# Two pairs of output-projection tiles by seven quarter products, in a hand-set order

## The chip, the cores and the metric

The kernel runs on one core of a Trainium2 chip. A core has five engines that work beside each other: TensorE (PE; its weight loads are listed apart as PEld), VectorE (DVE), ScalarE (ACT), GpSimd (POOL) and SyncE (SP), which here only issues DMA transfers. Each engine takes its own instructions in order and waits at semaphores for the others. The metric is device time in microseconds (us) of one execution; lower is better.

## The reference

One trunk layer of a decoder, on 512 prompt tokens and 8 x 8 sample tokens, 576 tokens in all, with a model width of 1024. What matters here is the middle of the layer:

```python
yb = o @ w_attn_out                                      # attention projection
mixed = jax.nn.sigmoid(ga) * ya + jax.nn.sigmoid(gb) * yb
x = x + g1 * (mixed @ w_mix_out)                         # output projection
h2 = _rmsnorm(x, norm2_g) * (1.0 + sc2) + sh2
a, val = jnp.split(h2 @ w_up, 2, axis=-1)                # first FFN product
```

`o` (the attention's output), `ya` (the other branch) and the gates `ga`, `gb` are there by then. The last parts of the adaLN modulation, `silu(c) @ w_ada`, from which `g1`, `sc2`, `sh2` and `g2` come, are still worked out beside the attention projection. All data are float32.

## The kernel before

Activations lie with the model width on the partitions, as 8 tiles of 128 x 576 tokens. Every float32 operand is split into a high and a low part (ACT copies the high part, rounded; DVE subtracts it for the low part), and a product takes three passes a k-step: high x high, high weights x low tokens, low weights x high tokens. Weight tiles are 128 output columns by the whole depth of 1024 (512 KB), loaded by SP into `raw` and split into `whi` and `wlo`. `W_BUFS` raw tiles and `S_BUFS` split ones are there at a time, and 57 general slots of 128 x 576 (`A_BUFS`) hold everything else.

A product of one tile comes in three forms:

- `product(w, xs)`: 8 k-steps of three passes, each in two matmuls of 256 and 320 columns (the token groups `GRP`), into one of the two `mm` PSUM tiles.
- `product_g(w, xs, g)`: the same for one token group, into one of the four `aux` PSUM tiles; it can call something between two k-steps.
- `pair_product`: two tiles at once. Weights and tokens are cut in halves (depth 512, 288 tokens), and seven products of a quarter take the place of eight, in the manner of Strassen and Winograd; each is a part of 4 k-steps x 3 passes of 288 columns. It needs sums of the weight halves (`pair_weights`, whose steps `sums1`, `ah`, `al` and so on make them one by one) and of the token halves (`PairOperands`: `sums`, `high`, `low`, `n3`), and further additions on the results. The gate projections before this stage and the FFN's up tiles from 4 on already run so; the output projection doesn't.

The order of the work is set in two ways. Where an engine's wrapper (`pe`, `act`, `dve`, `pool`) is in the list `pinned`, its instructions stay in program order. Elsewhere a scheduler orders them, by its own model of times. In the attention projection `pinned.clear()` frees everything after tile 3; `pinned.append(pe)` and, later, that of DVE and ACT at `NORM2[4]` bring the fixed order back. SP, the `load` helper aside, is never pinned here, and POOL's queue carries the two loads of x1.

The stages around the change, in order:

1. Attention projection: `product` of tiles 0 to 7 with the operands `o`. After each, DVE multiplies the result with the gate (`sg<-mm,sg`), adds `ya` (`sg<-sg,ya`), and the sum is split into `mxh` and `mxl`. In between, a filler (`fill`, `tick`) puts in the adaLN work: sides of 16 matmuls over 64 weight tiles `ada` of 256 KB, and at the end the transposes that bring the modulation to columns (`modT`).
2. Output projection, tiles 0 to 4: `product` with the operands `mixed`, each followed by `residual` (scaled by `g1`, added to `x1`) and `squares` (their sums over tiles go to `acc`, for the second norm). Among them are 22 small transposes of the FFN's convolution state.
3. Output projection, tiles 5 to 7, by groups (`mix_late`): group 0 of 5, 6, 7, then group 1 of 5, 6, 7, whose weights were split into general slots ahead (`late`). In group 1 of tile 5, behind k-step `NORM2[0]`, the row sums for the norm of group 0 are taken (`norm2_rows(0)`: DVE scales, POOL takes the root), and at k-step `NORM2[1]` of the next product their result is spread over the partitions (`spread_group`).
4. The FFN's start: the first up products, with the norm of group 1 put in.

Of the kernel before, what the change touches and what calls it, by code (L numbers as in the profile page):

```python
# [10 lines left out]
F32 = mybir.dt.float32  # L11
F32R = mybir.dt.float32r
# [4 lines left out]
P = 128  # L17
# [52 lines left out]
def step_kernel(ctx: ExitStack, tc: tile.TileContext, ins: dict, outs: list):  # L70
# [40 lines left out]

            return call

    pe, act, dve, pool = (InOrder(e) for e in (nc.tensor, nc.scalar, nc.vector, nc.gpsimd))
    pinned += [pe, act, dve, pool]
    matmul, transpose = pe.matmul, pe.transpose

# [27 lines left out]
    def load_w(src, nk):  # L145

        raw = wp.tile([P, nk, P], F32, tag="raw", name=nm("raw"), bufs=W_BUFS)
        nc.sync.dma_start(raw, src)
        return raw

    def split_w(raw):
        nk = raw.shape[1]
        hi = wp.tile([P, nk, P], F32R, tag="whi", name=nm("whi"), bufs=S_BUFS)
        lo = wp.tile([P, nk, P], F32R, tag="wlo", name=nm("wlo"), bufs=S_BUFS)
        split(hi, lo, raw)
        return (lambda k: hi[:, k, :]), (lambda k: lo[:, k, :])

    def split_w_slots(raw):

# [43 lines left out]
    def halves(ps):  # L203
        return ps[:, 256:512], ps[:, 512:832]

    def product(w, xs):
        ps = mmps()
        for k in range(len(xs)):
            kstep(halves(ps), w, xs, k)
            tick()  # L210
        return pf(ps)
# [17 lines left out]
    class PairOperands:  # L229

        def __init__(self, x, kp, made, values=None):
            self.x, self.kp = (x[kp], x[kp + 4]), kp
            self.r = values and (values[kp], values[kp + 4])
            self.made = made

        def sums(self):
            if not self.r:
# [11 lines left out]
        def high(self):  # L251
            made, (h0, l0), (h1, l1) = self.made, *self.x
            self.th, self.tl = slot("th", F32R), slot("tl", F32R)
            act.activation(self.th, self.t, AF.Copy)
            if self.kp % 2 == 0:
                made["n4"] = slot("nh", F32R), slot("nl", F32R)
            a, b = slice(0, HT), slice(HT, NT)
            at = (a, b)[self.kp % 2]
            nh, nl = made["n4"]
            self.nh, self.nl = nh[:, at], nl[:, at]  # L260
            act.activation(self.nh, self.r[0][:, a], AF.Copy)
            for name, hi, lo, c in (
                ("x00", h0, l0, a), ("n3", h0, l0, b), ("x10", h1, l1, a), ("x11", h1, l1, b),
                ("n1", self.th, self.tl, a), ("t2", self.th, self.tl, b), ("n4", nh, nl, at),
            ):
                made.setdefault("op", {}).setdefault(name, []).append((hi[:, c], lo[:, c]))

        def low(self):
            for lo, src, hi in ((self.tl, self.t, self.th), (self.nl, self.r[0][:, :HT], self.nh)):
                dve.tensor_tensor(out=lo, in0=src, in1=hi.bitcast(F32), op=ALU.subtract)  # L270

        def n3(self):

            (hi, lo), b = self.x[0], slice(HT, NT)
            split(hi[:, b], lo[:, b], self.r[0][:, b])

        def all(self):
            self.sums()
# [422 lines left out]
    def state_load(src, n):  # L701
        parts = []
        for m0 in range(0, n, 4):
            c = min(4, n - m0)
            s = slot("st", shape=[P, 512])
            load(s[:16, : c * P], src.rearrange("o b r c -> (o b r) c")[:, m0 * P : (m0 + c) * P])
            parts.append(s)
        return parts

# [413 lines left out]
    def modulation(c0):  # L1123

        ps = aux()
        cols = {}

        def rows(k):
            cols[k] = [slot("ada", shape=[P, 512]) for _ in range(4)]
            for j, t in enumerate(cols[k]):  # L1130
                c = c0 + 512 * j
                nc.sync.dma_start(t, ins["w_ada"][0, k * P : k * P + P, c : c + 512])
# [28 lines left out]
        yield False  # L1161
# [165 lines left out]

    def squares(xt, m, c0=0, c1=NT):
        if m == 0:
            nc.scalar.activation(acc[:, c0:c1], xt[:, c0:c1], AF.Square)  # L1330
        else:
            sq = slot("sq")
            nc.scalar.activation(sq[:, c0:c1], xt[:, c0:c1], AF.Square)
            nc.vector.tensor_tensor(
                out=acc[:, c0:c1], in0=acc[:, c0:c1], in1=sq[:, c0:c1], op=ALU.add
            )
# [4 lines left out]
    x1t = [wp.tile([P, 4, NT], F32, tag="oh", name=nm("x1"), bufs=2) for _ in range(2)]  # L1341
    for x in range(2):
        nc.gpsimd.dma_start(x1t[x], xT_dram[x])
    x1 = [x1t[k // 4][:, k % 4, :] for k in range(NK)]
    late = []
# [78 lines left out]
    mix_late(NK - 2, 1, (NORM2[1], first_parts))  # L1424
    mix_late(NK - 1, 1)


    w_up, w_dn = ins["w_up"][0], ins["w_down"][0]

    def ffn_conv(ps, m):  # L1430
        u = padded()
# [190 lines left out]
    def w_split(raw):  # L1622
        hi, lo = (wp.tile([P, NK, P], F32R, tag=t, name=nm(t), bufs=S_BUFS) for t in ("whi", "wlo"))
        act.activation(hi, raw, AF.Copy)
        low = lambda: dve.tensor_tensor(out=lo, in0=raw, in1=hi.bitcast(F32), op=ALU.subtract)
        return ((lambda k: hi[:, k, :]), (lambda k: lo[:, k, :])), low

    def start(t, ps):
        t.copies(ps)
# [225 lines left out]
```

## Time and profile before

| | |
|---|---|
| Median of 3 runs | 1000.4 us (1000.04 to 1001.07) |
| Profiled execution | 1001.41 us, span 999.6 us |
| Mean granted TensorE clock | 0.997 |
| PE busy | 983.2 us (98%) |
| DVE, ACT, POOL busy | 67%, 45%, 10% |
| HBM read, written | 109.17 MB, 7.35 MB |

The span runs from the first to the last recorded instruction; the device time is a little more. An engine's busy share over the whole span is an average over stages with different limits, so the stages are read one by one: the windows view gives each engine's busy time in a stretch, the timeline its instructions in order of time, the waits view who waited for whom. The columns of a timeline line are start, duration (of all that are merged), engine, line, operation, output<-inputs, count, and in brackets the idle time ahead and what ended it. Most operations go through a helper, so they carry its line, L109; they are told apart by the names of their tiles.

### The profile page before, as it was taken

The page shows a single profiled execution, that of the slowest core. Times are in us where ns is not written, and L with a number is a line of the kernel's source. Part 1 is how long each engine was busy: PE and PEld are TensorE (multiplying, and loading weights), DVE is VectorE, ACT ScalarE, POOL GpSimd, SP SyncE. Part 2 cuts the span into 40 slices and gives each one's busy share as a digit, 9 for nine tenths or more (in the row PEclk, how much of TensorE's full clock was granted, in tenths as well). Part 3 has the DMA queues.
Part 4 walks back from the last instruction along what each step waited for, and adds up shares of the span by engine and source line. Part 5 has one row for each costly group of instructions (what it writes and reads, how often), then busy time and mean ns, then how long its engine had stood idle before and what let it go on. Part 6 is the DMA issues. An engine that isn't in the chain of part 4 may idle for free.

```text
span 999.6 us, 18691 instructions
## 1 busy us (share of the span) xinstructions
PE 983.2 (98%) x7516; PEld 941.8 (94%) x7516; DVE 670.7 (67%) x1241; ACT 450.8 (45%) x835; POOL 100.3 (10%) x271
## 2 busy tenths in 40 slices
PE   7999999999999999999999999999999999999997
PEld 5899999999999989999889999999999999999997
DVE  5736676676463348788454568896569995579953
ACT  5454555545334225545232347554225552235453
POOL 2221101020000000000000021011001110001120
PEclk9999999999999999999999999999999999999999
DMA  9984332233421752235972302223233222323302
GB/s 290 319 253 109 86 90 70 86 116 115 141 76 53 246 180 85 86 106 157 338 231 72 106 11 75 65 85 106 85 101 90 85 85 86 106 65 101 110 10 95
DMA packets 173481, 119.18 MB, mean 119 GB/s; under 512 B 6887, under 2 KB 160846, under 8 KB 173106
## 3 DMA queue, kind: packets, MB, share of 16 engines
q1 hardware_dynamic: 169954, 107.00, 35.3%
q0 software_dynamic: 3296, 10.73, 3.5%
q8 instruction: 59, 0.97, 0.4%
q14 instruction: 28, 0.23, 0.1%
q10 hardware_dynamic: 144, 0.26, 0.1%
HBM read 109.17 MB, written 7.35 MB: 117 GB/s over the span
## 4 chain that ended last, share of the span: by engine, by line
PE 82%; DVE 10%; issue 2%; DMA 2%; ACT 2%; SPq 0%; POOL 0%; POOLq 0%; DVEq 0%; ACTq 0%
PE mm L109 60%; PE aux L109 19%; DVE wlo L109 3%; PE aux L1116 2%; DMA ad<-in_w_ada 2%; PE aux L1016 2%; DVE raw L109 1%; DVE uv L109 1%; DVE y L109 1%; DVE cy L109 1%; DMA raw<-in_w_in 1%; DVE fl L109 1%; SPq L385 0%; DVE wl L109 0%; ACT whi L109 0%
## 5 line engine op out<-in xcount | busy, mean ns | idle before, releaser
L109 ACT ACTIVATE whi<-raw 128x1024 fp32r<-128x1024 f32 (+2 forms) x164 | 168.1, 1034 | 178.6 <-PE mm L109 95.5
L109 DVE TENSOR_TENSOR wlo<-raw,whi 128x1024 fp32r<-128x1024 f32 (+2 forms) x164 | 195.1, 1194 | 48.6 <-ACT whi L109 47.9
L109 PE MATMUL mm<-hh,whi 128*128 128x256 f32 (+2 forms) x560 | 124.6, 299 | 0.6 <-ACT hh L109 0.6
L109 PE MATMUL mm<-hh,wlo 128*128 128x256 f32 (+2 forms) x560 | 121.8, 294 | 0.0
L109 PE MATMUL mm<-hl,whi 128*128 128x256 f32 (+2 forms) x560 | 121.0, 295 | 0.1
L109 PEld LDWEIGHTS mm<-hh,whi 128*128 128x128 f32 x560 | 93.0, 188 | 2.9 <-ACT hh L109 1.2
L109 PEld LDWEIGHTS mm<-hh,wlo 128*128 128x128 f32 x560 | 94.2, 188 | 0.0
L109 PEld LDWEIGHTS mm<-hl,whi 128*128 128x128 f32 x560 | 93.6, 188 | 0.5 <-DVE hl L109 0.5
L109 DVE SCALAR_TENSOR_TENSOR x<-mm,modT,x 128x512 f32<-128x512 f32 (+1 forms) x33 | 22.6, 686 | 71.1 <-PE mm L109 71.0
L109 PE MATMUL mm<-fh,whi 128*128 128x256 f32 (+1 forms) x304 | 65.0, 296 | 0.3 <-DVE rt L109 0.3
L109 PE MATMUL mm<-fl,whi 128*128 128x256 f32 (+1 forms) x304 | 65.1, 295 | 0.0
L109 PE MATMUL mm<-fh,wlo 128*128 128x256 f32 (+1 forms) x304 | 64.9, 295 | 0.0
L109 PE MATMUL mm<-th,whi 128*128 128x288 f32 x208 | 61.7, 297 | 0.7 <-DVE uv L109 0.7
L109 PE MATMUL mm<-th,wlo 128*128 128x288 f32 x208 | 61.6, 296 | 0.6 <-DVE wlo L109 0.6
L109 PE MATMUL mm<-tl,whi 128*128 128x288 f32 x208 | 61.4, 295 | 0.0
L109 PEld LDWEIGHTS mm<-fh,whi 128*128 128x128 f32 x304 | 50.7, 188 | 0.5 <-PE mm L109 0.5
L109 PEld LDWEIGHTS mm<-fl,whi 128*128 128x128 f32 x304 | 51.0, 188 | 0.0
L109 PEld LDWEIGHTS mm<-fh,wlo 128*128 128x128 f32 x304 | 50.8, 188 | 0.0
L867 ACT ACTIVATE s<-s,nmx 128x256 f32<-128x256 f32 (+1 forms) x72 | 34.0, 474 | 32.0 <-DVE nmx L864 31.2
L109 PE MATMUL aux<-2h,whi 128*128 128x288 f32 (+2 forms) x160 | 47.2, 295 | 0.8 <-ACT p L109 0.8
L109 PE MATMUL aux<-2h,wlo 128*128 128x288 f32 (+2 forms) x160 | 47.3, 296 | 0.0
L109 PE MATMUL aux<-2l,whi 128*128 128x288 f32 (+2 forms) x160 | 47.0, 294 | 0.0
(310 smaller groups left out, 2568.8 us busy)
## 6 DMA issues: line engine op xcount, KB each, us to landing
raw<-in_w_in SPq DMA_DIRECT2D x52, 512.0 KB, 4.2
raw<-in_w_up SPq DMA_DIRECT2D x44, 512.0 KB, 3.9
ada<-in_w_ada SPq DMA_DIRECT2D x64, 256.0 KB, 6.0
ad<-in_w_ada SPq DMA_DIRECT2D x32, 256.0 KB, 6.3
raw<-in_w_down SPq DMA_DIRECT2D x16, 512.0 KB, 3.5
raw<-in_w_conv_out SPq DMA_DIRECT2D x8, 512.0 KB, 3.5
raw<-in_w_attn_out SPq DMA_DIRECT2D x8, 512.0 KB, 4.2
raw<-in_w_mix_out SPq DMA_DIRECT2D x8, 512.0 KB, 6.1
```

Of the source, the lines that this page charges most:

```text
L109: done = getattr(self.engine, name)(*args, **kwargs)
L867: nc.scalar.activation(s[x // 2][:, x % 2, :w], s[x // 2][:, x % 2, :w], AF.Exp, bias=nmx[:, x : x + 1], accum_out=den[:, x : x + 1],)
L1016: done = nc.tensor.matmul(O[HALF[par], :256], vt(i - nkt + 1 + kt)[:, hd * 64 : hd * 64 + 64], pts[kt][:, par * 256 : par * 256 + 256], st ...
L1116: done = nc.tensor.matmul(ps[32 * j : 32 * j + 32, :], cT[:, k, :], cols[k][j], start=(k == 1), stop=(k == NK - 2),)
```

## The change

- The output projection's tile 0 stays a `product`, with its k-steps in the order 0, 4, 1, 5, 2, 6, 3, 7; the state's transposes come after it. Tiles 1, 2 and tiles 3, 4 become two calls of `pair_product` (`mix_pair`). Tiles 5 to 7 stay as they are.
- The attention projection takes its tiles in the order 0, 4, 1, 5, 2, 6, 3, 7, so that after every second one a pair (kp, kp + 4) of mixed tiles is there, whose sums, high and low parts are made at once, beside the next products. With `beside=True` the operand `n3` gets slots of its own, since the plain operands are still needed. The weights of pair (1, 2) are made there too, by the steps named in `PAIR_LOW` and `PAIR_HIGH`.
- The low half of each weight split is no longer made with its high half, but one or two products ahead of its use, ahead of the multiply that follows a product.
- PE, ACT, DVE and now SP stay pinned from there on; the scheduler orders nothing of this stretch any more. The filler's rate goes from 11/60 to 11/44.
- Squares, late weights and the first three FFN weights (`ws`) are put at set places: in the pairs' steps, in `mix_late`, and ahead of the group products.
- The loads of x1 move from POOL's queue to SP's, behind the state's loads and after the fifth attention product.
- `NORM2[0]` goes from 4 to 5.

TensorE issues 24 matmuls fewer (7066 to 7042 rows of its program), DVE 54 instructions more (1225 to 1279) and ACT 20 more (740 to 760). Up to the second attention product TensorE's order is the same; from the FFN's start on the order on every engine is the same too.

The core of the diff:

```diff
-NORM2 = 4, 0, 3, 1, 3
+NORM2 = 5, 0, 3, 1, 3
+PAIR_LOW = {2: "sums1", 3: "al", 4: "dl", 5: "sums2", 6: "bl"}
+PAIR_HIGH = {2: "ah", 3: "dh", 5: "bh", 6: "ch"}
...
+    def w_split(raw):
+        hi, lo = (wp.tile([P, NK, P], F32R, tag=t, name=nm(t), bufs=S_BUFS) for t in ("whi", "wlo"))
+        act.activation(hi, raw, AF.Copy)
+        low = lambda: dve.tensor_tensor(out=lo, in0=raw, in1=hi.bitcast(F32), op=ALU.subtract)
+        return ((lambda k: hi[:, k, :]), (lambda k: lo[:, k, :])), low
...
+            if self.beside:
+                if self.kp % 2 == 0:
+                    made["n3"] = slot("nh", F32R), slot("nl", F32R)
+                self.n3_parts = [y[:, at] for y in made["n3"]]
+                act.activation(self.n3_parts[0], self.r[0][:, b], AF.Copy)
...
         else:
             w_next[0] = weights(kpm(wao, 0), NK)
-            raw = load_w(kpm(wao, P), NK)
+            raw = load_w(kpm(wao, 4 * P), NK)
...
-    filler[1] = 11 / 60
-    mixed = []
-    for m in range(NK):
-        if m + 1 < NK and m + 1 not in w_next:
-            w_next[m + 1] = weights(kpm(wao, (m + 1) * P), NK)
-        ps = product(w_next.pop(m), o)
-        if m == 3:
-            pinned.clear()
-        t = gb[m]
+    pinned.append(sync)
+    filler[1] = 11 / 44
...
+    order = [m for kp in range(4) for m in (kp, kp + 4)]
+
+    def mixed_in(m, ps, between):
+        values[m] = t = gb[m]
         dve.tensor_tensor(out=t, in0=ps, in1=t, op=ALU.mult)
         dve.tensor_tensor(out=t, in0=t, in1=ya[m], op=ALU.add)
-        mixed.append(split_slot(t, "mx"))
+        mixed[m] = hi, lo = slot("mxh", F32R), slot("mxl", F32R)
+        act.activation(hi, t, AF.Copy)
+        for step in between:
+            step()
+        dve.tensor_tensor(out=lo, in0=t, in1=hi.bitcast(F32), op=ALU.subtract)
...
+    w_high(2)
+    for i, m in enumerate(order):
+        ps = product(w_next.pop(i), o)
+        if i + 2 in lows:
+            lows.pop(i + 2)()
+        if i == 1:
+            raws = [load_w(kpm(w_mix, c * P), NK) for c in (1, 2)]
+            w_pair, steps = pair_weights(*raws)
+            del raws
+        between = [steps[n] for n in PAIR_LOW.get(i, "").split()]
+        if i and i % 2 == 0:
+            between.append(op.low)
+        mixed_in(m, ps, between)
+        if i + 3 <= NK:
+            w_high(i + 3)
+        for n in PAIR_HIGH.get(i, "").split():
+            steps[n]()
+        if i % 2:
+            op = PairOperands(mixed, i // 2, made_mix, values, beside=True)
+            op.sums()
+            op.high()
+        if i == 4:
+            ffn_state = state_load(ins["state_ffn_conv"], NF)
+            x1t = [wp.tile([P, 4, NT], F32, tag="oh", name=nm("x1"), bufs=2) for _ in range(2)]
+            for x in range(2):
+                sync.dma_start(x1t[x], xT_dram[x])
+    op.low()
+    steps["cl"]()
     drain()
...
-    stF = state_in(state_load(ins["state_ffn_conv"], NF), "stF", NF)
...
-    for x in range(2):
-        nc.gpsimd.dma_start(x1t[x], xT_dram[x])
...
-    for m in range(NK - 3):
-        w = weights(kpm(ins["w_mix_out"][0], m * P), NK)
-        if m >= NK - 6:
-            late.append(split_w_slots(load_w(kpm(ins["w_mix_out"][0], (m + 3) * P), NK)))
-        residual(product(w, mixed), x1[m], 16 + m)
-        squares(x1[m], m)
+    ps = product(w_next.pop(NK), mixed, order)
+    stF = state_in(ffn_state, "stF", NF)
+    affine(A2, 32, 56, NK)
+    residual(ps, x1[0], 16)
+    w_pair2, steps = pair_weights(*raws)
+    steps = in_turn(steps)
+    steps[5] = lambda: squares(x1[0], 0)
+    steps[6] = lambda: late_weights(5)
+    mix_pair(w_pair, 1, 2, steps)
+    steps = {
+        1: lambda: squares(x1[1], 1), 2: lambda: late_weights(6), 3: lambda: squares(x1[2], 2),
+        4: lambda: late_weights(7), 5: lambda: ws.append(first_w()),
+    }
+    mix_pair(w_pair2, 3, 4, steps)
 
     def mix_late(m, g, between=None):
         ps = product_g(late[m - NK + 3], mixed, g, between=between)
+        if (m, g) == (NK - 3, 0):
+            squares(x1[3], 3)
+            squares(x1[4], 4)
+        if (m, g) == (NK - 3, 1):
+            ws.append(first_w())
...
     for m in range(NK - 3, NK):
         mix_late(m, 0)
-    pinned.append(pe)
+    ws.append(first_w())
     mix_late(NK - 3, 1, (NORM2[0], lambda: norm2_rows(0)))
...
-    ws = [weights(kpm(w_up, c * P), NK) for c in (0, NF, 1)]
...
-            pinned.extend([dve, act])
```

More of the change, by code (lines that the diff above doesn't have):

```diff
@@ L112, in __getattr__ @@
             return call
-    pe, act, dve, pool = (InOrder(e) for e in (nc.tensor, nc.scalar, nc.vector, nc.gpsimd))
+    pe, act, dve, pool, sync = (
+        InOrder(e) for e in (nc.tensor, nc.scalar, nc.vector, nc.gpsimd, nc.sync)
+    )
     pinned += [pe, act, dve, pool]
@@ L147, in load_w @@
         raw = wp.tile([P, nk, P], F32, tag="raw", name=nm("raw"), bufs=W_BUFS)
-        nc.sync.dma_start(raw, src)
+        sync.dma_start(raw, src)
         return raw
@@ L204, in halves, with product @@
         return ps[:, 256:512], ps[:, 512:832]
-    def product(w, xs):
+    def product(w, xs, order=None):
         ps = mmps()
-        for k in range(len(xs)):
+        for k in order or range(len(xs)):
             kstep(halves(ps), w, xs, k)
@@ L229, in step_kernel, with __init__ @@
     class PairOperands:
-        def __init__(self, x, kp, made, values=None):
+        def __init__(self, x, kp, made, values=None, beside=False):
             self.x, self.kp = (x[kp], x[kp + 4]), kp
             self.r = values and (values[kp], values[kp + 4])
-            self.made = made
+            self.made, self.beside = made, beside
         def sums(self):
@@ L260, in high @@
             self.nh, self.nl = nh[:, at], nl[:, at]
+            self.n3_parts = [y[:, b] for y in (h0, l0)]
+            if self.beside:
[3 more added lines that the diff above has]
+                act.activation(self.n3_parts[0], self.r[0][:, b], AF.Copy)
+            made.setdefault("op", {}).setdefault("n3", []).append(tuple(self.n3_parts))
             act.activation(self.nh, self.r[0][:, a], AF.Copy)
             for name, hi, lo, c in (
-                ("x00", h0, l0, a), ("n3", h0, l0, b), ("x10", h1, l1, a), ("x11", h1, l1, b),
+                ("x00", h0, l0, a), ("x10", h1, l1, a), ("x11", h1, l1, b),
                 ("n1", self.th, self.tl, a), ("t2", self.th, self.tl, b), ("n4", nh, nl, at),
@@ L268, in low @@
         def low(self):
-            for lo, src, hi in ((self.tl, self.t, self.th), (self.nl, self.r[0][:, :HT], self.nh)):
+            parts = [(self.tl, self.t, self.th), (self.nl, self.r[0][:, :HT], self.nh)]
+            if self.beside:
+                parts.append((self.n3_parts[1], self.r[0][:, HT:], self.n3_parts[0]))
+            for lo, src, hi in parts:
                 dve.tensor_tensor(out=lo, in0=src, in1=hi.bitcast(F32), op=ALU.subtract)
         def n3(self):
-            (hi, lo), b = self.x[0], slice(HT, NT)
-            split(hi[:, b], lo[:, b], self.r[0][:, b])
+            if not self.beside:
+                split(*self.n3_parts, self.r[0][:, HT:])
         def all(self):
@@ L705, in state_load @@
             s = slot("st", shape=[P, 512])
-            load(s[:16, : c * P], src.rearrange("o b r c -> (o b r) c")[:, m0 * P : (m0 + c) * P])
+            sync.dma_start(s[:16, : c * P], src.rearrange("o b r c -> (o b r) c")[:, m0 * P : (m0 + c) * P])
             parts.append(s)
@@ L1329, in squares @@
         if m == 0:
-            nc.scalar.activation(acc[:, c0:c1], xt[:, c0:c1], AF.Square)
+            act.activation(acc[:, c0:c1], xt[:, c0:c1], AF.Square)
         else:
             sq = slot("sq")
-            nc.scalar.activation(sq[:, c0:c1], xt[:, c0:c1], AF.Square)
-            nc.vector.tensor_tensor(
+            act.activation(sq[:, c0:c1], xt[:, c0:c1], AF.Square)
+            dve.tensor_tensor(
                 out=acc[:, c0:c1], in0=acc[:, c0:c1], in1=sq[:, c0:c1], op=ALU.add
@@ L1336, in squares @@
             )
-    stF = state_in(state_load(ins["state_ffn_conv"], NF), "stF", NF)
     A2 = cp.tile([P, NK, 9], F32, tag="A2", name="A2")
-    affine(A2, 32, 56, NK)
-    x1t = [wp.tile([P, 4, NT], F32, tag="oh", name=nm("x1"), bufs=2) for _ in range(2)]
-    for x in range(2):
-        nc.gpsimd.dma_start(x1t[x], xT_dram[x])
-    x1 = [x1t[k // 4][:, k % 4, :] for k in range(NK)]
-    late = []
-    for m in range(NK - 3):
-        w = weights(kpm(ins["w_mix_out"][0], m * P), NK)
-        if m >= NK - 6:
-            late.append(split_w_slots(load_w(kpm(ins["w_mix_out"][0], (m + 3) * P), NK)))
-        residual(product(w, mixed), x1[m], 16 + m)
-        squares(x1[m], m)
+    x1 = [x1t[k // 4][:, k % 4, :] for k in range(NK)]
@@ new lines, in step_kernel, with first_w, late_weights, mix_pair @@
+    late, ws = [], []
+    w_up, w_dn = ins["w_up"][0], ins["w_down"][0]
+    def first_w():
+        return weights(kpm(w_up, (0, NF, 1)[len(ws)] * P), NK)
+    raws = [load_w(kpm(w_mix, c * P), NK) for c in (3, 4)]
+    def late_weights(m):
+        late.append(split_w_slots(load_w(kpm(w_mix, m * P), NK)))
+    def mix_pair(w, ma, mb, steps):
+        def out(m, c0, c1):
+            def done(x, y, op):
+                dve.tensor_tensor(out=y, in0=x, in1=y, op=op)
+                residual(y, x1[m], 16 + m, c0, c1)
+            return done
+        def a0(ps):
+            residual(ps, x1[ma], 16 + ma, 0, HT)
+        pair_product(w, made_mix["op"], steps, a0, out(ma, HT, NT), out(mb, 0, HT), out(mb, HT, NT))
@@ L1425, in step_kernel @@
     mix_late(NK - 1, 1)
-    w_up, w_dn = ins["w_up"][0], ins["w_down"][0]
     def ffn_conv(ps, m):
@@ L1620, in step_kernel @@
     ops = [PairOperands(h2, kp, made2, h2_raw) for kp in range(4)]
[L1622 to L1626, printed above, removed]
     def start(t, ps):
```

9 lines of the change are left out of this document (8 added, 1 removed).

## The prediction

> **What bounds the kernel now.** I read the page's first part (busy time by engine) and fourth part (the chain that ended last), then the windows view of the stages that the change touches. The page:
>
> ```profile
> PE 983.2 (98%) x7516; PEld 941.8 (94%) x7516; DVE 670.7 (67%) x1241; ACT 450.8 (45%) x835; POOL 100.3 (10%) x271
> ...
> PE 82%; DVE 10%; issue 2%; DMA 2%; ACT 2%; SPq 0%; POOL 0%; POOLq 0%; DVEq 0%; ACTq 0%
> ```
>
> The windows view over the attention projection, the five full products of the output projection, its first group and its second group up to the first FFN product's end (columns: window, length, busy time of PE, PEld, DVE, ACT, POOL, granted clock, DMA share, GB/s):
>
> ```profile
> 479.90:534.30 54.40, 54.40 (x407) 46.98 (x406) 27.65 (x34) 15.40 (x19) 0.00 (x0) 1.00 0.72 241
> 534.30:567.70 33.40, 33.40 (x262) 33.03 (x261) 17.02 (x28) 10.93 (x16) 0.00 (x0) 1.00 0.36 105
> 567.70:587.70 20.00, 20.00 (x155) 20.00 (x154) 10.57 (x27) 4.27 (x9) 2.62 (x8) 1.00 0.05 14
> 587.70:606.80 19.10, 19.10 (x147) 18.96 (x147) 17.25 (x52) 14.66 (x38) 6.05 (x12) 1.00 0.19 56
> ```
>
> TensorE is busy for all of every stage, at granted clock 1.00: time can be won only by giving it less, and is lost wherever another engine lets it wait. DVE, to which the change gives work, is busy for 44.67 of the first 87.8 us, and nearly always (17.25 of 19.1) only at the FFN's start, where the order stays as it is. After the FFN's start every engine's order is unchanged, with TensorE as the bound, so what is won or lost up to there shifts the end by as much.
>
> **Step 1, the pairs: -3.10 us.** A full product is 24 matmuls of 256 columns and 24 of 320. The timeline of TensorE at tile 4's product: from 561.39 exactly 24 passes to the first group product (the rows between are one pass each):
>
> ```profile
> 561.39 0.43 PE L109 MATMUL mm<-mxh,whi 128*128 128x256 f32 x2
> ...
> 567.73 0.28 PE L109 MATMUL aux<-mxh,wh 128*128 128x256 f32 x1
> ```
>
> That is 6.34 us, and two products 12.68. The same seven quarter products of 12 matmuls of 288 columns run in the gate projections; the timeline of one such pair, its first part, its second, and the next pair's first:
>
> ```profile
> 437.53 0.29 PE L109 MATMUL mm<-hh,whi 128*128 128x288 f32 x1
> ...
> 439.12 0.29 PE L109 MATMUL aux<-hh,whi 128*128 128x288 f32 x1
> ...
> 448.67 0.29 PE L109 MATMUL mm<-hh,whi 128*128 128x288 f32 x1
> ```
>
> A part is 1.59 us and the pair 11.14. So a pair saves 12.68 - 11.14 = 1.54 to 1.55, and two pairs 3.10. The operands and weights that this needs are priced in step 3.
>
> **Step 2, the attention projection in fixed order: -1.18 us.** The DVE timeline gives each product's end by its first reader (`sg<-mm,sg`):
>
> ```profile
> 479.95 0.76 DVE L109 TENSOR_TENSOR sg<-mm,sg 128x576 f32<-128x576 f32 x1 [1.14 <-PE mm L109]
> 480.74 0.76 DVE L109 TENSOR_TENSOR sg<-sg,ya 128x576 f32<-128x576 f32 x1
> ...
> 488.36 0.76 DVE L109 TENSOR_TENSOR sg<-mm,sg 128x576 f32<-128x576 f32 x1 [3.87 <-PE mm L109]
> ...
> 496.77 0.76 DVE L109 TENSOR_TENSOR sg<-mm,sg 128x576 f32<-128x576 f32 x1 [3.88 <-PE mm L109]
> ...
> 500.07 3.50 DVE L109 TENSOR_TENSOR wlo<-raw,whi 128x1024 fp32r<-128x1024 f32 x3 [0.19 <-ACT whi L109]
> 503.49 0.75 DVE L109 TENSOR_TENSOR sg<-mm,sg 128x576 f32<-128x576 f32 x1
> ...
> 512.72 0.76 DVE L109 TENSOR_TENSOR sg<-mm,sg 128x576 f32<-128x576 f32 x1 [4.68 <-PE mm L109]
> ...
> 519.08 0.76 DVE L109 TENSOR_TENSOR sg<-mm,sg 128x576 f32<-128x576 f32 x1 [3.01 <-PE mm L109]
> ...
> 527.92 0.76 DVE L109 TENSOR_TENSOR sg<-mm,sg 128x576 f32<-128x576 f32 x1 [0.21 <-PE mm L109]
> ...
> 534.28 0.76 DVE L109 TENSOR_TENSOR sg<-mm,sg 128x576 f32<-128x576 f32 x1 [3.00 <-PE mm L109]
> ```
>
> A product alone takes 6.36 (512.72 to 519.08, and the last); with one side of 16 adaLN matmuls 8.41. From 496.77 to 512.72 there are two products and one side, 14.77, but 15.95 passed: 1.18 too many. The cause is the order that the scheduler chose: it put three splits of output-projection weights (3.50 us) ahead of the split that the fifth attention product needs. TensorE's timeline and the waits view there:
>
> ```profile
> 503.57 1.90 PE L1116 MATMUL aux<-ada,cT 128*32 128x512 f32 x10
> ...
> 505.86 1.06 PE L1116 MATMUL aux<-ada,cT 128*32 128x512 f32 x6
> ```
> ```profile
> PEld mm L109 <- DVE wlo L109: 0.8, 1, 0.8
> ```
>
> The wait of 0.8 is one part of it, the side broken into 10 and 6 the rest. In the changed order each product's low weights are made a product ahead, and with the side rate 11/44 each side falls whole behind products 0, 1, 2, 3. The last product then ends at 534.28 - 1.18 = 533.1. Bounds: 0, if another wait takes its place, and 1.18; I take 1.18, as the three other sides show what an unbroken side takes (8.41 twice; 8.84 once, with 0.43 of transposes that remain).
>
> **Step 3, what is added.** 116 DVE instructions lie between the first attention product's end and the first group product: 32 of 576 columns, 38 of 288, 17 of 512, 13 of 1024 and 16 small. The groups view prices them:
>
> ```profile
> L109 DVE TENSOR_TENSOR wlo<-raw,whi 128x1024 fp32r<-128x1024 f32 x14 | 16.9, 1221 | 1.5 <-ACT whi L109 1.4
> L109 DVE TENSOR_TENSOR sg<-sg,ya 128x576 f32<-128x576 f32 x8 | 6.1, 757 | 0.2
> ...
> L109 DVE TENSOR_TENSOR wl<-raw,wh 128x512 fp32r<-128x512 f32 x6 | 3.9, 685 | 0.0
> ```
> ```profile
> L109 DVE TENSOR_TENSOR uv<-mm,p 128x288 f32<-128x288 f32 x15 | 6.8, 453 | 2.1 <-PE mm L109 1.7
> ```
>
> 32 x 0.757 + 38 x 0.453 + 17 x 0.685 + 13 x 1.221, and about 4.5 for the small ones, is 73.5 us, in 83.6 us of TensorE time. 39.8 of it lies within the 53.2 us of the attention projection and hides there. The rest, 60 instructions and 33.7 us, lies in the stretch from 533.1 to the first group product: one full product 6.34, 22 state transposes (1.41 + 0.29 below), two pairs 22.28, together 30.3 us.
>
> ```profile
> 540.64 1.41 PE L109 MATMUL aux<-ident,st 16*128 16x16 f32 x20
> ...
> 542.32 0.29 PE L109 MATMUL aux<-ident,st 16*128 16x16 f32 x2
> ```
>
> Instructions in a row overlap by some 0.08 us (three splits of 1.221 in 3.50); dependent ones don't. So DVE needs about 30.5 us there: it is full, and what it leaves is caught up beside the group products, where it now works 10.57 of 20 us. Followed in the hand-set order with these durations, the last pair operand and weight part come some 2 us ahead of pair (1,2)'s second part; the closest place is the third part of pair (3,4), whose PSUM bank is freed by a subtraction queued behind two splits of late weights, 0.3 to 0.5 us ahead. I take that as nothing, plus 0.1 for a bank that comes just late.
>
> Queues: the two loads of x1 stood on POOL's queue (tile view):
>
> ```profile
> L1343 POOL DMA_DIRECT2D x<-xT_dram x2: 532/550/567, 474.9 to 479.1; - x2
> ...
> DMA to landing us min/median/max: 8.6/9.0/9.4
> ```
>
> They move to SP's, behind the state loads and the attention weights, at about 507; with 9.4 us they land by 517 to 519 and are first read near 541 (533.1 + 6.34 + 1.7). The state loads, small, are wanted at about the same time, so neither costs anything; if that cover were gone, TensorE would wait only through PSUM banks, a part later. NORM2's first entry puts the row sums one k-step later, and on DVE a split (1.221) stands ahead of the scaling that follows, where now an idle 1.13 stands:
>
> ```profile
> 578.97 0.16 DVE L109 TENSOR_SCALAR r<-aux 128x2 f32<-128x2 f32 x1 [1.13 <-PE aux L109]
> ```
>
> That costs between 0 and 0.45 (one k-step's time) with 0.1 of split; I take 0.15, near the lower end, since one later entry is unmoved and had room.
>
> **Sum.** -3.10 - 1.18 + 0.10 + 0.15 = -4.03. The profiled execution took 1001.41 for a span of 999.6; it would be 997.4, with a span of 995.6. It lies 1.0 above the median of 1000.4 (1000.04 to 1001.07), which becomes **996.4**.
>
> **Rivals.**
>
> *A: the last adaLN tile comes late.* The side behind product 3 starts at 505.2 and wants the last of 64 tiles. Its load waits on SP until DVE has read out its slot: product 2's end 496.77, multiply, add, two sums for the weights, then the token operand, about 3.7 us, so issue at 500.5; queued behind it on SP are two attention weights, due from 520 on, and the state and x1 loads. Landing times, in three windows of the tile view (465 to 468, 480 to 520, 463 to 480):
>
> ```profile
> DMA to landing us min/median/max: 4.0/4.5/5.0
> ```
> ```profile
> DMA to landing us min/median/max: 4.4/6.0/6.2
> ```
> ```profile
> DMA to landing us min/median/max: 4.0/7.2/12.1
> ```
>
> With 4.0 it lands at 504.5, in time; with 6.0 at 506.5, TensorE waits 1.3; with 12.1 it waits 7.4. I take 4.0 to 4.5: six of its group of eight have gone by then, and the 6.0 were eight in a row. With 6.0 the time is 997.7. [...]
>
> *B: only the matmuls go.* The wait of step 2 comes back at another place of the new order: 1000.4 - 3.10 = 997.3.
>
> *C, the slower one: DVE holds TensorE in the stretch of step 3.* Everything there is in fixed order, and 19 of the 60 instructions wait for ScalarE's half of a split or a square. Such waits now, in the gate stage:
>
> ```profile
> DVE wlo L109 <- ACT whi L109: 8.1, 17, 1.4
> ```
>
> That is 0.48 each. If none of the 19 is hidden, DVE needs 9.1 us more and, past the 0.4 of margin, TensorE waits 8.7: -4.0 + 8.7 = +4.7, 1005.1. It ends slower than before from 4.4 us, nine or ten such waits, and by over 2 us from about fourteen. Against it: ScalarE has 10.93 of 33.4 us to do there now, and the high halves are set a product or a part ahead. One to three of the waits uncovered belong to my own range (up to +1.0). [...]
>
> *E: DVE instructions don't overlap.* At their full durations the 60 need 33.7 us where 30.5 and the margin of 0.4 are to be had: TensorE waits 2.8, and 996.4 + 2.8 = 999.2. For it speak the dependent ones (the multiply at 479.95 takes 0.76, and the add on its result starts at 480.74); against it the three splits in 3.50 us. [...]
>
> *D: no change.* Matmuls leave, and waits of 3 to 5 us spread over the stretch replace them: 1000.4.
>
> **How the numbers follow.** Forecast 0.58, A 0.13, B 0.10, C 0.09, D 0.05, E 0.05. A measurement of this kernel tells about 0.2%, 2 us, from no change. Faster by more (under 998.4): the forecast, nearly all of A, and B, 0.80. Within 2 us: D, E, and the near part of C, 0.11. Slower by more: the rest of C, and A with a landing of 12 us, 0.09. The range runs from 995.3 (all of step 2 at no cost, 996.1; the 0.4 by which the fastest run lies under the median; and 0.4 for gains of order that I don't see, the size of the smallest broken piece above) up to E's 999.2, through A and B, and leaves out C and D, 0.14.
>
> **What would show it.** In the profile after, the first reads of the attention products should stand 8.4 apart three times after the first, hence 505.2 for the fourth, and the last near 533.1 (step 2); each new pair should take 11.1 us from first to first (step 1); the first group product should start near 563.4, 4.3 earlier, and the FFN's first product end near 583.6. A shows as a wait of TensorE's loads for `ada` at 505; C as waits of `mm` or `aux` for DVE between 533 and 564, with DVE over 95% busy. I am wrong if TensorE's busy time falls by 3 us and the span does not follow, or if the pairs take more than 11.6 us each.

## The result, and the profile after

The changed kernel takes 997.38 us (median of 6 runs, 996.94 to 998.08) against 1000.4 (6 runs): ratio 0.9968, interval 0.9957 to 0.9979, so 2.1 to 4.3 us less. Measured again on another occasion, it was 997.54 against 1000.88, ratio 0.9967 (0.9955 to 0.9980). The profiled execution took 997.27 us with a span of 995.5, clock 0.997.

The DVE timeline after, first reads of the eight attention products (the first four and the last):

```profile
479.24 0.75 DVE L111 TENSOR_TENSOR sg<-mm,sg 128x576 f32<-128x576 f32 x1
...
487.63 0.76 DVE L111 TENSOR_TENSOR sg<-mm,sg 128x576 f32<-128x576 f32 x1 [3.87 <-PE mm L111]
...
496.04 0.76 DVE L111 TENSOR_TENSOR sg<-mm,sg 128x576 f32<-128x576 f32 x1 [2.54 <-PE mm L111]
...
504.44 0.76 DVE L111 TENSOR_TENSOR sg<-mm,sg 128x576 f32<-128x576 f32 x1 [2.32 <-PE mm L111]
...
532.37 0.76 DVE L111 TENSOR_TENSOR sg<-mm,sg 128x576 f32<-128x576 f32 x1 [1.60 <-PE mm L111]
```

TensorE's timeline after: the first matmul of pair (3,4), of the first group product, and of the FFN:

```profile
551.36 0.29 PE L111 MATMUL aux<-mxh,whi 128*128 128x288 f32 x1
...
562.53 0.28 PE L111 MATMUL aux<-mxh,wh 128*128 128x256 f32 x1
...
583.44 0.28 PE L111 MATMUL mm<-2h,whi 128*128 128x256 f32 x1
```

The FFN's start before, and ScalarE's first copy of an FFN product before and after:

```profile
587.67 0.28 PE L109 MATMUL mm<-2h,whi 128*128 128x256 f32 x1
```
```profile
606.81 0.70 ACT L109 COPY pad<-mm 128x512 f32<-128x512 f32 x2 [0.92 <-PE mm L109]
```
```profile
602.53 0.70 ACT L111 COPY pad<-mm 128x512 f32<-128x512 f32 x2 [1.35 <-PE mm L111]
```

These marks cut the stretch into stages, all in us; "order only" is the first experiment below.

| Stage | Before | After | Difference | Order only |
|---|---|---|---|---|
| first to last attention read | 54.33 | 53.13 | -1.20 | 53.15 |
| to the first group product | 33.45 | 30.16 | -3.29 | 33.19 |
| to the FFN's first matmul | 19.94 | 20.91 | +0.97 | 20.88 |
| to the FFN's first copy | 19.14 | 19.09 | -0.05 | 19.06 |
| sum | 126.86 | 123.29 | -3.57 | 126.28 |

The two spans differ by 4.1, but 0.71 of that stands ahead of the change, where the programs are the same (the first read at 479.95 and 479.24; in the runs below it lies anywhere from 479.0 to 480.5). The change's own worth in these traces is 3.57 us. A second trace of the changed kernel gives 123.31 for the same stretch, so the marks repeat far better than the times do.

The windows view after, stage by stage, tells where a wait was added:

```profile
479.90:533.40 53.50, 53.50 (x409) 47.27 (x409) 37.27 (x58) 18.41 (x27) 0.00 (x0) 1.00 0.72 234
533.40:563.60 30.20, 30.20 (x240) 30.01 (x239) 26.71 (x51) 13.48 (x23) 0.00 (x0) 1.00 0.37 104
563.60:583.60 20.00, 19.38 (x147) 19.12 (x146) 14.32 (x34) 6.78 (x12) 3.44 (x7) 1.00 0.29 82
583.60:602.70 19.10, 19.10 (x148) 18.92 (x147) 17.41 (x53) 14.61 (x39) 6.66 (x13) 1.00 0.19 56
```

TensorE is full but for the third row: 0.62 us of idle time lie among the group products, where before there was none. (The stage is 0.97 longer. From the last matmul ahead of the spread to the spread it is 0.93 where it was 0.14, and from there to the next product's matmul 0.47 where it was 0.37, 0.89 in all, start to start.) The wait is for POOL, at the norm's first spread:

```profile
576.26 0.71 PE L111 MATMUL aux<-ident,r 128*128 128x128 f32 x4 [0.62 <-POOL r L111]
```

POOL's power, before and after:

```profile
579.21 0.73 POOL L109 TENSOR_TENSOR r<-r,mhalf 128x2 f32<-128x2 f32 x1 [99.56 <-DVE r L109]
```
```profile
574.57 1.63 POOL L111 TENSOR_TENSOR r<-r,mhalf 128x2 f32<-128x2 f32 x1 [247.22 <-DVE r L111]
```

The same instruction takes 0.90 us longer. Two things differ beside it: DVE runs a split of 1.21 us just then, and POOL had been idle for 247 us and not 100:

```profile
574.33 0.15 DVE L111 TENSOR_SCALAR r<-aux 128x2 f32<-128x2 f32 x1
574.40 1.21 DVE L111 TENSOR_TENSOR wlo<-raw,whi 128x1024 fp32r<-128x1024 f32 x1
```

### The profile page after: what moved, and what is told of

The parts are those of the page before. It is cut to its first block, busy times and chain, and to the rows that moved or that the text cites. A ratio compares the mean times of both kernels' runs of the same rounds, so it can differ in the third digit from the quotient of the medians.

```text
span 995.5 us, 18728 instructions
## 1 busy us (share of the span) xinstructions
PE 978.1 (98%) x7492; PEld 938.8 (94%) x7492; DVE 695.0 (70%) x1295; ACT 459.7 (46%) x855; POOL 100.6 (10%) x269
## 4 chain that ended last, share of the span: by engine, by line
PE 60%; issue 27%; DVE 8%; ACT 2%; DMA 1%; POOL 1%; SPq 0%; POOLq 0%; DVEq 0%; ACTq 0%
PE mm L111 43%; PE aux L111 15%; DVE wlo L111 2%; PE aux L1037 2%; DVE raw L111 1%; DMA x<-in_x_prompt 1%; DVE uv L111 1%; DVE y L111 1%; DVE cy L111 1%; ACT whi L111 0%; DVE fl L111 0%; DVE wl L111 0%; DVE s L111 0%; ACT y L111 0%; DVE tl L111 0%
## 5 line engine op out<-in xcount | busy, mean ns | idle before, releaser
L111 ACT ACTIVATE whi<-raw 128x1024 fp32r<-128x1024 f32 (+2 forms) x166 | 170.1, 1034 | 151.4 <-PE mm L111 83.9
L111 DVE TENSOR_TENSOR wlo<-raw,whi 128x1024 fp32r<-128x1024 f32 (+2 forms) x166 | 197.7, 1194 | 48.3 <-ACT whi L111 47.8
L111 PE MATMUL mm<-th,whi 128*128 128x288 f32 x224 | 66.3, 296 | 0.6 <-DVE uv L111 0.5
L111 PE MATMUL mm<-th,wlo 128*128 128x288 f32 x224 | 66.4, 296 | 0.6 <-DVE wlo L111 0.6
L111 PE MATMUL mm<-tl,whi 128*128 128x288 f32 x224 | 66.1, 295 | 0.0
L111 DVE SCALAR_TENSOR_TENSOR x<-mm,modT,x 128x512 f32<-128x512 f32 (+1 forms) x29 | 19.6, 676 | 57.7 <-PE mm L111 57.5
```

Source lines behind the costliest of these rows:

```text
L111: done = getattr(self.engine, name)(*args, **kwargs)
```

## The experiments

The totals are from the first attention read to the FFN's first copy (before 126.86, after 123.29); a median time stands beside a total where a kernel ran several times. Five kernels (one more power on POOL, the loads of x1 on POOL's queue, the old side rate, and the two with more work for DVE) ran once, in the profiled execution, and are judged by their totals alone.

**Order without pairs.** Tiles 1 to 4 are full products, in the hand-set order.

```diff
-    mix_pair(w_pair, 1, 2, steps)
...
-    mix_pair(w_pair2, 3, 4, steps)
+    for m in range(1, NK - 3):
+        ps = product(w, mixed)
...
```

> The changed kernel with the attention projection and all loads in its hand-set order, but tiles 1 to 4 as full products and no pair operands or pair weights. My account: the eight attention products take 53.1 us from the first read of the first to the first read of the last, as in the changed kernel (54.3 before), tiles 0 to 4 take as long as before, 33.3 to 33.5 us, and the wait of about 0.6 us for POOL's power ahead of the norm's spread is there too, since the up weights are split at the same places. So about 1.2 less, 0.9 more: 0.1 to 0.5 us under before, no difference that the times can tell. Rival, that the order alone brings the gain and the pairs nothing: 3 us faster than before, like the changed kernel.

Measured: ratio 0.9998 (0.9989 to 1.0007), total 126.28. The attention projection takes 53.15, so all of the 1.20 comes from the order. The next stage is 0.26 under before without any pair. The likely reason is that the state's transposes no longer break a product (22 in one row of 1.53 us; before, 1.41 and 0.29 within a product), but no run separates it. The pairs themselves are worth 33.19 - 30.16 = 3.03. The 0.94 lost among the group products is there too, so it belongs to the order, not to the pairs.

**Pairs without the order.** The pairs, with operands and weights placed by the scheduler.

```diff
         mixed.append(split_slot(t, "mx"))
+        if m >= 4:
+            op = PairOperands(mixed, m - 4, made_mix, gb, beside=True)
+            op.sums()
+            op.high()
+            op.low()
...
-        residual(product(w, mixed), x1[m], 16 + m)
+        mix_pair(w, n, n + 1, {})
```

> The kernel before, with its attention projection and its scheduler, but tiles 1 to 4 as two pairs, their operands and weights placed by the scheduler. My account: the 24 matmuls go (3.1 us), but nothing makes the operands beside the attention projection in time, so TensorE waits ahead of pair (1,2) or inside the pairs for DVE, by more than it saves: at least 3 us of waits in that stretch, time equal to before or slower, 1000 to 1006 us. Rival, that the scheduler finds a good order and only the matmul count matters: 3 us faster than before, 997.3, with no wait over 0.5 us between the last attention product and the first group product.

Measured: ratio 1.0103 (1.0089 to 1.0116), 1010.99 us, total 138.84: 12 us more, about twice the most I had expected. The timeline of TensorE and the windows around it:

```profile
545.13 0.61 PE L109 MATMUL aux<-nh,whi 128*128 128x288 f32 x1 [2.02 <-ACT whi L109]
563.46 0.61 PE L109 MATMUL aux<-nh,whi 128*128 128x288 f32 x1 [5.27 <-ACT whi L109]
```
```profile
546.00:552.00 6.00, 6.00 (x37) 6.00 (x38) 3.89 (x5) 1.78 (x2) 0.00 (x0) 0.79 0.74 217
...
564.00:570.00 6.00, 6.00 (x33) 6.00 (x32) 5.80 (x9) 2.31 (x4) 0.00 (x0) 0.59 0.47 138
```

The waits (2.0, 5.3, and 1.5 later for the norm's sums) are 8.8 us; the rest is the clock: after each of them it is down to half, so that a 6 us window without a wait, at a mean granted clock of 0.79 and 0.59, holds 37 and 33 matmuls where others at 1.00 hold 47 to 50. The order is what makes the pairs pay.

**POOL's power by itself.** One more power on a scratch tile, 3 us ahead.

```diff
         mix_late(m, 0)
+        if m == NK - 2:
+            pool.tensor_tensor(out=r2w, in0=acc[:, 0:2], in1=mhalf[:, 0:2], op=ALU.pow)
```

> The changed kernel with one more power of 128x2 elements on POOL, on a scratch tile, some 3 us ahead of the one that the norm needs. Theory 1 (DVE's split beside it makes the power long): the needed power still takes about 1.6 us and TensorE waits about 0.6 us ahead of the spread. Theory 2 (POOL's long idle time makes the first one long): the scratch power takes about 1.6 us, the needed one about 0.75, and the wait is gone.

```profile
572.06 0.72 POOL L111 TENSOR_TENSOR r2w<-acc,mhalf 128x2 f32<-128x2 f32 x1 [243.45 <-DVE acc L111]
...
575.83 1.60 POOL L111 TENSOR_TENSOR r<-r,mhalf 128x2 f32<-128x2 f32 x1 [3.05 <-DVE r L111]
```

Measured: the scratch power takes 0.72 after 243 us of idle time, the needed one still 1.60 after 3 us, and TensorE waits 0.6 as before (total 123.23). Idle time is not the cause.

**The up weights' splits placed otherwise.** Four placements. In the first, the second and third splits go ahead of the residuals of tiles 6 and 7 in group 0:

```diff
-        if (m, g) == (NK - 3, 1):
+        if (m, g) in ((NK - 2, 0), (NK - 1, 0)):
             ws.append(first_w())
...
-    ws.append(first_w())
```

> The changed kernel with the second and third up weights split one and two group products earlier, so that DVE has no split ahead of or behind the scaling that POOL's power waits for. Theory 1 (the power takes 1.63 us instead of 0.73 because DVE runs a split of 1.2 us beside it): the power takes about 0.75 us, TensorE's wait of 0.6 us ahead of the spread is gone, and the FFN's start comes 0.6 to 0.9 us earlier against the first group product than in the changed kernel; time about 996.5 to 996.8. Theory 2 (it takes 1.63 because POOL had computed nothing for 247 us): the power still takes about 1.6 us and the wait stays within 0.1 us; time as the changed kernel.

```profile
576.64 0.72 POOL L111 TENSOR_TENSOR r<-r,mhalf 128x2 f32<-128x2 f32 x1 [249.09 <-DVE r L111]
```
```profile
575.75 0.61 PE L111 MATMUL aux<-ones,acc 128*128 128x2 f32 x4 [1.69 <-DVE acc L111]
```
```profile
573.00:577.30 4.30, 2.61 (x19) 2.35 (x18) 2.20 (x4) 0.56 (x2) 0.66 (x1) 1.00 0.75 216
577.30:580.70 3.40, 3.40 (x16) 3.40 (x15) 2.56 (x8) 1.38 (x3) 1.62 (x7) 0.53 0.07 19
```

With no split beside it the power takes 0.72, after 249 us of idle time: theory 1 holds. But the time is 999.12 (ratio to before 0.9982, 0.9973 to 0.9991), total 125.92. The splits now stand ahead of the last residual, the row sums come late, TensorE waits 1.69, and from 1.5 us after that wait it runs 3.4 us at a clock of 0.53. In the second placement the third split goes one product later:

```diff
-        if (m, g) == (NK - 3, 1):
+        if (m, g) == (NK - 2, 1):
             ws.append(first_w())
```

> The changed kernel with the split of the third up weights moved one product later, behind the norm's first parts, so that no split stands beside POOL's power; the second up weights' split stays where it is. My account: the power takes about 0.73 us instead of 1.63, TensorE's wait of 0.6 us ahead of the spread goes, and the norm's second part is late by at most 0.2 us: from the first attention product's first read to the FFN's first copy 122.5 to 122.9 us (123.3 in the changed kernel), 0.4 to 0.8 us faster than the changed kernel. Rival: the split, now ahead of the residual of tile 6, makes the second group's sums late, TensorE waits there instead, and the time is that of the changed kernel or worse.

```profile
574.96 0.73 POOL L111 TENSOR_TENSOR r<-r,mhalf 128x2 f32<-128x2 f32 x1 [247.23 <-DVE r L111]
...
586.15 0.80 PE L111 MATMUL aux<-ones,acc 128*128 128x2 f32 x6 [0.90 <-DVE acc L111]
```

The power takes 0.73, there is no wait for POOL, and the stage of the group products takes 20.02 where it took 20.91: 0.89 of the 0.97 lost there came from the split beside the power. But the total is 123.33, the time 997.65 us. The rival came about: TensorE waits 0.9 for DVE's sums of the second group. In the third placement the second split goes ahead of tile 6's residual and the third where the second was:

```diff
-        if (m, g) == (NK - 3, 1):
+        if (m, g) == (NK - 2, 0):
             ws.append(first_w())
```

> The changed kernel with the second and third up weights each split one group product earlier: the second in the idle time of DVE between two residuals of group 0, the third where the second was, so that no split is left beside POOL's power, and, other than with both moved further ahead, none ahead of the last residual of group 0, nor (as with the third moved back) ahead of tile 6's. My account: the power takes 0.73 us, no wait of TensorE over 0.3 us from the first group product to the FFN's first copy, that stretch 0.6 to 0.9 us shorter than in the changed kernel (first attention read to FFN's first copy 122.4 to 122.7 us, 123.3 now). Rival: one more split ahead of the sums again makes them late, and the wait for DVE takes the place of the wait for POOL: 123.2 us or more.

The power takes 0.73, but DVE's scaling ahead of it stands behind the split and comes later: TensorE waits 0.6 as before, the total is 123.46, the time 997.78 us. The fourth placement is the second with the norm of group 1 shifted:

```diff
-NORM2 = 5, 0, 3, 1, 3
+NORM2 = 5, 0, 3, 2, 4
```

> The changed kernel with the third up weights' split behind the norm's first parts (no split beside POOL's power, as in the run that had this alone), and the row sums and the spread of the norm's second group each one step later in the FFN's start (1.08 us, three products of a step), so that the sums that the moved split delays by 0.9 us are there in time. My account: neither the wait for POOL nor that for DVE is left, and from the first attention product's first read to the FFN's first copy it takes 122.4 to 122.8 us, against 123.3 in the changed kernel: 0.5 to 0.9 us faster, 996.7 to 997.1 by the median of the changed kernel. Rival: DVE is without idle time in the FFN's start, so the later spread makes the second group's parts late, TensorE waits there, and nothing is won.

Now, too, the stage of the group products is 20.02 (20.91 after). The next is 19.99 (19.09), and the waits view names the reason:

```profile
PEld mm L111 <- DVE 2l L111: 1.0, 3, 0.6
```

Total 123.32, 997.31 us. Four placements, and no total under the 123.29 of the changed kernel. DVE is busy for 14.32 of the 20 us of the group products and for 17.41 of 19.1 behind them; in each of these four places the split made something late, and its place only set who waits. That no other place would do better is not shown.

**The loads of x1 back on POOL's queue.**

```diff
-                sync.dma_start(x1t[x], xT_dram[x])
+                nc.gpsimd.dma_start(x1t[x], xT_dram[x])
```

> The changed kernel with the two loads of x1 back on POOL's queue. My account: no difference, from the first attention product's first read to the FFN's first copy 123.2 to 123.4 us, since on either queue they land 20 us before they are read; POOL's power still takes 1.6 us, with a shorter idle time of POOL ahead of it. Rival (on POOL they go out at 475 to 479, among the attention weights and adaLN tiles, and slow these): a wait of TensorE's loads for an adaLN tile or attention weights of 0.5 us or more between 480 and 510.

```profile
501.22 2.72 PE L1137 MATMUL aux<-ada,cT 128*32 128x512 f32 x16 [3.17 <-DMA ada<-in_w_ada]
```
```profile
L111 SPq DMA_DIRECT2D ada<-in_w_ada x16: 328/374/1368, 489.5 to 502.6; - x16
```

Measured: total 128.53, 5.24 us longer; the rival held, not my account. The last sixteen tiles go out from 489.5 to 502.6, against 482.9 to 499.6 in the changed kernel, and TensorE waits 3.7 us in all, followed by 3.4 us at half clock (0.65 from 501.2 to 504.5 and 0.84 from there to 508 as means). POOL's power takes 1.64 here, after 101 us of idle time, about as long as before the change (99.56).

**The adaLN sides at the old rate.**

```diff
-    filler[1] = 11 / 44
+    filler[1] = 11 / 60
```

> The changed kernel with the adaLN sides spread as before the change (rate 11/60 for 11/44), so that they fall within products and not behind them. If the 1.18 us of the attention projection were the late weight split alone (0.8) and the broken sides (0.4), then the eight products take 53.1 us as now plus up to 0.4 for the broken sides, no wait for a weight split. Rival (the sides' place is all of it): 54.3 us as before the change.

```profile
528.20 0.74 PE L111 MATMUL aux<-ident,row 128*128 128x128 f32 x4 [3.38 <-ACT row L1167]
```

Measured: total 128.29, attention projection 58.31: neither expectation. The modulation's transposes now fall within the seventh product, and the ScalarE copy that they read stands behind weight splits that wait 2.82 us for a load. So this does not split the 1.20 into its two parts; it shows that in a fixed order the place of the filler's work, here of the transposes at its end, is worth 5 us.

**More work for DVE.** The two subtractions for tile 5's late weights are done twice, and four times.

```diff
             split(hi, lo, raw[:, k0 : k0 + n, :])
+            if again:
+                dve.tensor_tensor(
+                    out=lo, in0=raw[:, k0 : k0 + n, :], in1=hi.bitcast(F32), op=ALU.subtract
+                )
```

> The changed kernel with DVE's two subtractions for the late weights of tile 5 done twice, 1.28 us more DVE work just ahead of the subtraction that frees the PSUM bank of pair (3,4)'s third part. If the margin there is 0.3 us, as the prediction had it and the trace of the changed kernel shows (bank free at 554.29, taken at 554.58), TensorE waits 0.9 to 1.1 us for DVE ahead of that part. Rival (the bank is not what binds, DVE has some 3 us of idle time in the stretch): no wait.

Done twice, 1.28 us more work: TensorE waits 1.1 us, and the total is 124.60, 1.3 more. The margin is the 0.2 to 0.3 that the trace shows.

> The changed kernel with the two subtractions for the late weights of tile 5 done four times each, 3.85 us more DVE work at the place where 1.28 us gave a wait of 1.1. By the margin alone TensorE waits 3.6 to 3.8 us there, and the first group product comes 3.6 to 3.8 us later than in the changed kernel. If waits of this size also bring the clock down, as the 2.0 and 5.3 us of the scheduler's pairs did (one and two windows of 3.41 us at half clock) and the 1.1 us did not, one window at half clock follows and the stretch is 5.3 to 5.5 us longer.

```profile
554.00:560.00 6.00, 2.03 (x13) 1.78 (x13) 5.76 (x11) 0.17 (x1) 0.00 (x0) 0.88 0.02 6
560.00:566.00 6.00, 6.00 (x28) 6.00 (x28) 3.75 (x8) 4.70 (x8) 0.00 (x0) 0.55 0.53 153
```

Measured: the wait is 4.0, 0.2 over what the margin gives, and the total 130.29, 7.0 more. 28 matmuls in six full microseconds, at a mean granted clock of 0.55, and 0.88 in the six ahead of them: the clock was at half for 6.8 us, twice as long as expected.

**The changed kernel again.**

> The changed kernel unaltered, beside the others on the same chip: 3 to 4 us faster than before, as its trace gives 3.6 us between the first attention product and the FFN's first copy.

Measured: 997.54 us, total 123.31, as told above.

## Why the prediction was right, and where it was not

The forecast was 996.4 in 995.3 to 999.2, faster; measured 997.38. The sum was -4.03, the stretch gives -3.57 and the times -3.0 (-2.1 to -4.3). The median is also what rival B gave, 997.3, but not by B's way: the 1.2 us that B denies came, and 0.97 went elsewhere.

- **Step 1, the pairs, -3.10.** Shown: 3.03, by the run without them. A pair takes 11.17 (551.36 to 562.53), against 11.14 forecast.
- **Step 2, the order of the attention projection, -1.18.** Shown: 1.20 with pairs or without, and reads 8.4 apart at the forecast places. That the wait for one weight split is 0.8 of it and the broken side 0.4 was read off the trace and not separated by a run.
- **The state's transposes, at nothing.** The stage without pairs is 0.26 shorter than before, most likely by them.
- **Step 3, DVE in the stretch of the pairs.** It needed 30.5 in my count. It runs from 532.37 to 565.6, of which 3 us are waits for other engines, so 30.3 (29.6 by the busy time of the windows view); it ends behind the first group product, as forecast, and TensorE never waits. The margin of 0.3 to 0.5 at the bank of pair (3,4) was 0.2 to 0.3: the rival C was that near, and E (no overlap, 2.8 us) did not come.
- **The norm's first entry, +0.15.** This is the term that was mis-sized: 0.97. I bounded it by a k-step and by the split ahead of DVE's scaling, at 0.45 and 0.1; the scaling was indeed only 0.1 late. The split behind it was left out, and it stretched POOL's power from 0.73 to 1.63. The power took 0.72 to 0.73 us in the kernel before and in the four placements, which have no split beside it, and 1.60 to 1.64 in seven runs that have one (the changed kernel twice, one more power on POOL, x1 on POOL's queue, the old side rate, and the two with more work for DVE). With the later entry but no split beside the power the stage loses 0.08 (20.02 against 19.94), within my bounds. No run puts the entry back to 4 in the new order; that would leave the long power one k-step (0.44) more of room, if the sums are there by then.
- **The loads of x1, at nothing.** The size was right, but the reason was half: I only asked whether x1 itself would be early enough. The last adaLN tile went out at 499.6 and its side began at 505.13 without a wait, so A did not come. With x1 left on POOL's queue, waits for adaLN tiles came (3.7 us), but one product earlier than A had them: the first of the last sixteen tiles went out at 489.5 (482.9 in the changed kernel), the last at 502.6. What held them on SP's queue is not shown. In this order the move is worth 5.2 us.
- **The prices of the rivals.** I charged a wait of TensorE once. In these runs those of 1.5 to 5.3 us cost more than their length, since 3.4 to 6.8 us at half clock came with them; if C's 8.7 us had come in such waits, C was priced too low. No run shows C's nineteen waits.

The profiled execution, 997.27, lies nearer the 997.4 given for it than the terms deserve: 0.71 of its 4.14 is a difference ahead of the change, which by luck made up for most of the 0.97.

## What to carry to other kernels

Fewer matmuls pay only if their operands are there: the same pairs cost 12 us in the scheduler's order and gained 3 in one where each split, sum and load has its place. Where an engine has little idle time at the places that count, moving its work about may only change who waits, as it did in the four placements here; look for the engine without slack before the next change of place. When DVE and POOL stand in one chain, ask what DVE runs beside POOL's instruction, not only what it runs ahead of it; and when a load is moved to another queue, ask which other loads it was beside.

## What the hardware showed that was not expected

**A wait of TensorE of 1.21 us was followed by 3.4 us at about half its clock, and one of 1.86 us was not.** In the stretch above, single waits of 0.6, 0.9 and 1.1 us (the changed kernel, the third split one product later, the subtractions done twice) left the clock at 1.00. After waits of 1.5 and 2.0 us (the pairs without the order), 1.7 (the first placement), 3.2 (x1 on POOL's queue) and 3.4 us (the old side rate) it was at half for about 3.4 us, which at that clock costs another 1.7, half of it; around those of 4.0 (the subtractions done four times) and 5.3 us (the pairs without the order) for 6.8 us, begun within the wait. But there is one more wait, near 16 us from the start (`aux<-ident,rs`, for POOL). In the kernel before it is 1.55 us and in the changed kernel 1.50, each followed by 3.4 us at 0.50. In two other kernels, the one with one more power on POOL and the one with the third split one product later, it came out differently; each is shown with the windows view of the 3.4 us in question (the granted clock is the third number from the right):

```profile
15.34 0.88 PE L111 MATMUL aux<-ident,rs 128*128 128x128 f32 x6 [1.21 <-POOL rs L111]
```
```profile
16.10:19.50 3.40, 3.40 (x27) 1.19 (x26) 2.03 (x3) 0.95 (x2) 0.00 (x0) 0.54 1.11 339
```
```profile
16.86 0.88 PE L111 MATMUL aux<-ident,rs 128*128 128x128 f32 x6 [1.86 <-POOL rs L111]
```
```profile
16.90:20.30 3.40, 3.21 (x30) 1.52 (x30) 2.03 (x3) 0.95 (x2) 0.00 (x0) 1.00 1.11 362
```

A granted clock of 0.54 followed the wait of 1.21 us, and 1.00 that of 1.86. So its length alone does not decide; what else does, such as where a wait falls, these runs do not show.

**POOL's power beside DVE's split took 1.60 to 1.64 us in place of 0.73**, while the split kept its length (1.21 to 1.22 us beside the power, 1.22 to 1.23 ahead of it in the last three placements): of the two, POOL alone was held up. In six of the seven runs (all but the one with one more power on POOL) the power ended 0.57 to 0.59 us after the split. If it runs at its usual pace once the split is over, most of its 0.73 us of work was done then; that is an estimate from these two figures. What in the split holds POOL up no run shows.
